# HGRN scores of each level as products of 64 or 32 keys with their own queries

## The chip, the cores and the metric

The kernel runs on one core of a Trainium2 chip. The metric is the device time of one execution in microseconds, as the median of several runs. Before the change it is 2824.28 us (three runs, 2824.19 to 2826.57).

## What is computed

A trunk of two layers over 256 tokens of 2048 features in float32: a gated DeltaNet layer, a SwiGLU feed-forward layer, an HGRN2 layer and a second feed-forward layer. The change lies in the HGRN2 token mixer, in the scores of its chunks:

```python
# q, k, logf: (B,S,H,dk), 16 heads of 128; chunks of 64 tokens
qc, kc, vc = to_chunks(q), to_chunks(k), to_chunks(v.astype(jnp.float32))
Bc = jnp.cumsum(to_chunks(logf), axis=-2)
def step(S, inp):
    q_c, k_c, v_c, b_c, qd_c, kd_c, fl_c = inp
    dec = jnp.exp(jnp.where(causal, b_c[..., :, None, :] - b_c[..., None, :, :], -jnp.inf))
    scores = jnp.einsum("bhid,bhjd,bhijd->bhij", q_c, k_c, dec)
    o = jnp.einsum("bhid,bhde->bhie", qd_c, S) + jnp.einsum("bhij,bhje->bhie", scores, v_c)
    S = S * fl_c[..., :, None] + jnp.einsum("bhjd,bhje->bhde", kd_c, v_c)
    return S, o
```

The decay differs by channel, so a score is not a plain product of a query and a key; it needs a factor in each channel that depends on both positions.

## The kernel before

**The stream of weights.** All weights pass through the core once, in half chunks of 128x1024. SP loads a half (`raw`), ScalarE rounds it (`wh`), VectorE takes the rest (`wl`), and TensorE multiplies three products of the parts with the activations. These matmuls write the PSUM tiles `main`. Four buffers each hold `raw`, `wh` and `wl`.

**The work beside it.** The token mixers' own matmuls are in plain float32 and write PSUM tiles `aux`, of which there are four (one bank each). The profile shows a float32 matmul as two pairs of a weight load and a matmul; such a pair is called a record below. The page gives most instructions one line, L489, since a recording layer issues them; so they are told apart by their tiles.

**What sets the order.** The program is recorded first. A planner (`Recorder.plan`) then places operations engine by engine: the stream's matmuls keep their order, and the other matmuls are put between them when their operands should be ready by a table of costs (`COST`, `PE_SLACK`, `FP32_PRODUCT`). `batches` keeps the matmuls of one `aux` tile, or of tiles declared `together`, in one piece. Each engine then runs its instructions in that order.

**HGRN scores.** The 16 heads come in four groups of four. For a group, `hgrn_scores` takes the 256 tokens as two blocks of 128 per head (eight pairs of head and block). Pairs of a later query and an earlier key are covered by levels `s` = 64, 32, 16, 8, 4, 2 and 1: at level `s` a block of 2s tokens has its keys in the first half and its queries in the second, and with `b` at the last key as reference both factors are plain exponentials. `products` makes `kp` (keys times the factor), `qp` (queries times the factor) and one matmul for each head and block of 128. At levels 64 and 32 the keys are packed to 64 columns; at levels 16, 8, 4 and 2 all 128 keys are multiplied with all 64 queries. `keep` copies what belongs together into `sc` (keys in partitions, eight blocks, queries): ScalarE by slices at levels 64 and 32, VectorE with a mask (`copy_predicated`) below. Level 1 and the diagonal (each query with its own key) come from one product of 128 keys with 64 + 128 columns `q_last`, in four `aux` tiles. `hgrn_o` multiplies `v` by `sc`.

Two levels form one piece for the planner, so a group has three stretches on TensorE: levels 64 and 32; levels 16 and 8; levels 4, 2 and 1 with the diagonal.

Of the kernel before, what the change touches and what calls it, by code (L numbers as in the profile page):

```python
# [11 lines left out]
AF = mybir.ActivationFunctionType  # L12
ALU = mybir.AluOpType
# [4 lines left out]
P = 128  # L18
T = 256
D = 2048  # L20
EPS = 1e-6
CH = 64
# [3 lines left out]
N_HGRN = 4  # L26
LEVELS = (64, 32, 16, 8, 4, 2, 1)
MASKED = LEVELS[2:]
AHEAD = 3
RAW_BUFS = 4  # L30
SPLIT_BUFS = 4
# [474 lines left out]
class Trunk:  # L506
# [79 lines left out]
    def stream(self, groups):  # L586
# [10 lines left out]
        def load(n):  # L597
            g, i = flat[n]
            raw = self.tile(self.wraw, [P, 1024], "raw", ordered=True)
            nc.sync.dma_start(raw, g.halves[i])  # L600
            if n == 0:
                nc.ops[-1].lag = 4.2
                nc.edge(self.queue[1], nc.ops[-1])
            h = place("wh", g)
            nc.scalar.activation(h, raw, AF.Copy)
            low = place("wl", g)
            nc.vector.tensor_tensor(out=low, in0=raw, in1=h.bitcast(F32), op=ALU.subtract)
            ready[n] = (h, low)

        loaded = 0  # L610
        for n, (g, i) in enumerate(flat):
            while loaded < min(n + AHEAD, len(flat)):
                load(loaded)
# [730 lines left out]
    def hgrn_setup(self):  # L1344
# [4 lines left out]
        nc.gpsimd.dma_start(self.hgrn_hn, a["hgrn_hn"])  # L1349
        self.masks = t([P, len(MASKED), CH], "masks", U8)  # L1350
        raw = self.tile(self.pool, [P, len(MASKED), CH], "e", bufs=2, ordered=True)
        nc.gpsimd.dma_start(raw, a["masks"])
# [56 lines left out]
    def hgrn_scores(self, g, q, st):  # L1409
        nc = self.nc  # L1410
        t = lambda shape, tag, **kw: self.tile(self.pool, shape, tag, **kw)
        b, k = st["b"], st["k"]
        e = t([P, 4, T], "e", bufs=2, ordered=True)
        nc.scalar.activation(e, q, AF.Tanh, scale=0.5)
        nc.vector.scalar_tensor_tensor(
            out=q, in0=e, scalar=1.0, in1=q, op0=ALU.add, op1=ALU.mult
        )
        tt = lambda out, in0, in1, op: nc.vector.tensor_tensor(out=out, in0=in0, in1=in1, op=op)
        halves = lambda x, s: x.rearrange("p h (n t s) -> p (h n) t s", t=2, s=s)
        flat = lambda x: x.rearrange("p h t -> p (h t)")  # L1420


        e, kp, qp = t([P, 4, T], "e", bufs=2, ordered=True), self.kp[0], t([P, 4, P], "qp", bufs=2, ordered=True)
        ch = lambda x, c: x[:, :, c * CH : (c + 1) * CH]
        tot = lambda c: b[:, :, (c + 1) * CH - 1 : (c + 1) * CH].broadcast_to([P, 4, CH])
        tt(ch(e, 0), tot(0), ch(b, 0), ALU.subtract)
        tt(ch(e, 0), ch(e, 0), tot(1), ALU.add)
        tt(ch(e, 1), tot(1), ch(b, 1), ALU.subtract)
        nc.vector.tensor_copy(ch(e, 2), ch(b, 2))
        tt(ch(e, 3), ch(b, 3), tot(2), ALU.add)  # L1430
        nc.scalar.activation(e, e, AF.Exp)
        tt(kp[:, :, 0:P], k[:, :, 0:P], e[:, :, 0:P], ALU.mult)
        tt(qp, q[:, :, P:T], e[:, :, P:T], ALU.mult)
        ps = self.aux()
        for h in range(4):
            nc.tensor.matmul(
                ps[:, h * P : (h + 1) * P], kp[:, h, 0:P], qp[:, h, :], start=True, stop=True
            )
        cross = t([P, 512], "cross")
        nc.scalar.activation(cross, ps, AF.Copy)  # L1440
        st["cross"] = cross

        sc = t([P, 8, P], "sc")
        nc.gpsimd.memset(sc, 0.0)

        def products(n, s, ps):
            e, qp = t([P, 4, T], "e", bufs=2, ordered=True), t([P, 4, P], "qp", bufs=2, ordered=True)
            bv, ev, kv, qv = (halves(x, s) for x in (b, e, k, q))
            m, whole, kp = 512 // s, s not in MASKED, self.kp[(n + 1) % 2]
            if whole:  # L1450
                kp = flat(kp)[:, 0:512]
                left = kp.rearrange("p (m s) -> p m s", s=s)
            else:
                left = halves(kp, s)[:, :, 0, :]
            ref = bv[:, :, 0, s - 1 : s].broadcast_to([P, m, s])
            tt(ev[:, :, 0, :], ref, bv[:, :, 0, :], ALU.subtract)
            if s == CH:
                nc.scalar.activation(ev[:, :, 0, :], ev[:, :, 0, :], AF.Exp)
                nc.scalar.activation(ev[:, :, 1, :], bv[:, :, 1, :], AF.Exp)
            else:  # L1460
                tt(ev[:, :, 1, :], bv[:, :, 1, :], ref, ALU.subtract)
                nc.scalar.activation(e, e, AF.Exp)
            tt(left, kv[:, :, 0, :], ev[:, :, 0, :], ALU.mult)
            tt(qp.rearrange("p h (n s) -> p (h n) s", s=s), qv[:, :, 1, :], ev[:, :, 1, :], ALU.mult)
            for h in range(4):
                for tok in range(2):
                    at = (2 * h + tok) * CH
                    keys = kp[:, at : at + CH] if whole else kp[:, h, tok * P : (tok + 1) * P]
                    nc.tensor.matmul(
                        ps[0 : CH if whole else P, at : at + CH], keys,  # L1470
                        qp[:, h, tok * CH : (tok + 1) * CH], start=True, stop=True,
                    )

        def keep(n, s, ps):
            pv = ps.rearrange("p (a n s) -> p a n s", a=8, s=s)
            if s not in MASKED:
                for i in range(CH // s):
                    nc.scalar.activation(
                        sc[2 * i * s : (2 * i + 1) * s, :, (2 * i + 1) * s : (2 * i + 2) * s],
                        pv[i * s : (i + 1) * s, :, i, :], AF.Copy,  # L1480
                    )
            else:
                nc.vector.copy_predicated(
                    sc.rearrange("p a (n t s) -> p a n t s", t=2, s=s)[:, :, :, 1, :],
                    self.masks[:, n - 2, :].rearrange("p (n s) -> p n s", s=s).unsqueeze(1)
                    .broadcast_to([P, 8, CH // s, s]),
                    pv,
                )

        for n in range(0, len(LEVELS) - 1, 2):  # L1490
            two = self.aux(), self.aux()
            nc.together(*two)
            for step in (products, keep):
                for i in range(2):
                    step(n + i, LEVELS[n + i], two[i])


        e, qp = t([P, 4, T], "e", bufs=2, ordered=True), t([P, 8, CH + P], "q_last")
        pairs = lambda x: x.rearrange("p h (a n t) -> p (h a) n t", a=2, t=2)
        bv, ev, qv = (pairs(x) for x in (b, e, q))  # L1500
        nc.gpsimd.tensor_copy(qp[:, :, CH:], q.rearrange("p h (a t) -> p (h a) t", t=P))
        tt(ev[:, :, :, 1], bv[:, :, :, 1], bv[:, :, :, 0], ALU.subtract)
        nc.scalar.activation(ev[:, :, :, 1], ev[:, :, :, 1], AF.Exp)
        tt(qp[:, :, 0:CH], qv[:, :, :, 1], ev[:, :, :, 1], ALU.mult)
        mask = lambda m: m.unsqueeze(1).broadcast_to([P, 2, m.shape[1]])
        pv = []
        for h in range(4):
            if h % 2 == 0:
                two = self.aux(), self.aux()
                nc.together(*two)  # L1510
            pv.append(two[h % 2][:, 0 : 2 * (CH + P)].rearrange("p (a i) -> p a i", a=2))
            for tok in range(2):
                nc.tensor.matmul(
                    pv[h][:, tok, :], k[:, h, tok * P : (tok + 1) * P], qp[:, 2 * h + tok, :],
                    start=True, stop=True,
                )
        for h in range(4):
            out = sc[:, 2 * h : 2 * h + 2, :]
            nc.vector.copy_predicated(
                out.rearrange("p a (n t) -> p a n t", t=2)[:, :, :, 1],  # L1520
                mask(self.masks[:, len(MASKED) - 1, :]), pv[h][:, :, 0:CH],
            )
            nc.vector.copy_predicated(out, mask(self.same), pv[h][:, :, CH:])
        st["sc"] = sc

    def hgrn_o(self, g, st):
# [128 lines left out]
def layout(inputs):  # L1655
# [33 lines left out]
    def out_rows(w):  # L1689
# [20 lines left out]
    out["masks"] = np.stack(  # L1710
        [((j >= c // s * 2 * s) & (j < c // s * 2 * s + s)).astype(np.float32) for s in MASKED], 1
    )
# [21 lines left out]
```

## Time and profile before

| What | Value |
|---|---|
| median of three runs | 2824.28 us |
| the profiled execution's own time | 2823.72 us |
| its span on the page | 2822.0 us |
| granted TensorE clock | 0.999 |
| DMA moved | 580.46 MB, 206 GB/s in the mean |
| SyncE and GpSimd | POOL busy 253.7 us; the loads' queue 53.9% of the DMA engines' span |
| HGRN stage | 1574 to about 2000 us of the span |

An instruction row of the timeline is: start in us, length in us, engine, line, operation, output tile <- input tiles, array tile (rows*columns), shape, and how many alike follow each other. The length of such a run ends with its last record's own latency, so starts are compared rather than ends. In a group row the busy time is a union, behind it the mean length in ns.

### The profile page before, as it was taken

The numbers are of one execution on the slowest core, as the hardware profiler recorded it, in microseconds if no ns is written. First come the engines' busy times: TensorE is split into PE (matmuls) and PEld (weight loads), VectorE is DVE, ScalarE is ACT, GpSimd is POOL, SyncE is SP. The second block draws the span as 40 slices with busy tenths as digits, with TensorE's granted clock in tenths as the row PEclk, the third lists the DMA queues.
The fourth block names the chain that finished last, engine by engine and source line by source line (L and its number), as shares of the span: only waits on it lengthen the run. The fifth ranks groups of instructions, "written<-read, shape, count | busy, mean of one in ns | idle before, by whom it ended". The sixth has DMA issues, their size and how long they took to land.

```text
span 2822.0 us, 39791 instructions
## 1 busy us (share of the span) xinstructions
PE 2806.4 (99%) x15198; PEld 2398.8 (85%) x15198; DVE 1745.9 (62%) x2511; ACT 1420.5 (50%) x1972; POOL 253.7 (9%) x370
## 2 busy tenths in 40 slices
PE   9999999999999999999999999999999999999998
PEld 9988888888888888888888989999888888888887
DVE  6787888877665545445555677677565455445554
ACT  6646666564554444344444555556454444344443
POOL 1212222222110000000000100000110000000000
PEclk9999999999999999999999999999999999999999
DMA  7686668668676555665556644544685556665554
GB/s 258 194 277 205 205 221 260 213 206 267 229 254 196 187 192 188 223 224 187 193 187 224 209 151 165 165 150 165 223 268 187 193 188 204 225 205 193 187 198 160
DMA packets 162672, 580.46 MB, mean 206 GB/s; under 512 B 20138, under 2 KB 21306, under 8 KB 162352
## 3 DMA queue, kind: packets, MB, share of 16 engines
q1 hardware_dynamic: 138912, 503.15, 53.9%
q0 software_dynamic: 23280, 73.91, 8.3%
q8 instruction: 119, 1.95, 0.3%
q10 hardware_dynamic: 288, 0.85, 0.1%
q14 instruction: 73, 0.60, 0.1%
HBM read 550.52 MB, written 27.31 MB: 205 GB/s over the span
## 4 chain that ended last, share of the span: by engine, by line
PE 98%; ACT 0%; DVE 0%; issue 0%; DMA 0%; SPq 0%; POOLq 0%; POOL 0%; ACTq 0%
PE main L489 90%; PE aux L489 8%; ACT dec L489 0%; DMA first<-in_x 0%; DVE wl L489 0%; DVE u L489 0%; ACT wh L489 0%; DVE utmp L489 0%; DVE pre L489 0%; SPq L489 0%; ACT xt_h L489 0%; ACT y L489 0%; POOLq L1730 0%; ACT junk L489 0%; DVE xl L489 0%
## 5 line engine op out<-in xcount | busy, mean ns | idle before, releaser
L489 DVE TENSOR_TENSOR wl<-raw,wh 128x1024 fp32r<-128x1024 f32 x945 | 1162.3, 1231 | 973.9 <-ACT wh L489 971.4
L489 ACT ACTIVATE wh<-raw 128x1024 fp32r<-128x1024 f32 x945 | 1000.6, 1060 | 1287.1 <-PE main L489 1238.9
L489 PE MATMUL main<-wh,xt_h 128*128 128x512 f32 x2176 | 850.7, 391 | 0.6 <-ACT wh L489 0.6
L489 PE MATMUL main<-wl,xt_h 128*128 128x512 f32 x2176 | 849.2, 390 | 0.9 <-DVE wl L489 0.9
L489 PE MATMUL main<-wh,xt_l 128*128 128x512 f32 x2176 | 849.4, 390 | 0.0
L489 PEld LDWEIGHTS main<-wl,xt_h 128*128 128x128 f32 x2176 | 408.7, 188 | 84.3 <-DVE wl L489 1.3
L489 PEld LDWEIGHTS main<-wh,xt_h 128*128 128x128 f32 x2176 | 408.7, 188 | 84.2 <-ACT wh L489 1.0
L489 PEld LDWEIGHTS main<-wh,xt_l 128*128 128x128 f32 x2176 | 408.7, 188 | 83.6
L489 PE MATMUL main<-xt_h,wl 128*128 128x256 f32 (+1 forms) x1040 | 292.3, 281 | 1.1 <-DVE wl L489 1.1
L489 PE MATMUL main<-xt_l,wh 128*128 128x256 f32 (+1 forms) x1040 | 291.9, 281 | 0.3 <-DVE xt_l L489 0.3
L489 PE MATMUL main<-xt_h,wh 128*128 128x256 f32 (+1 forms) x1040 | 290.1, 279 | 0.0
L489 PE MATMUL main<-wh,hth 128*128 128x512 f32 x664 | 258.7, 390 | 0.0
L489 PE MATMUL main<-wh,htl 128*128 128x512 f32 x664 | 258.6, 389 | 0.0
L489 PE MATMUL main<-wl,hth 128*128 128x512 f32 x664 | 258.4, 389 | 0.0
L489 PEld LDWEIGHTS main<-xt_h,wh 128*128 128x128 f32 (+1 forms) x1040 | 195.7, 188 | 0.3
L489 PEld LDWEIGHTS main<-xt_h,wl 128*128 128x128 f32 (+1 forms) x1040 | 193.8, 186 | 1.6 <-DVE wl L489 1.5
L489 PEld LDWEIGHTS main<-xt_l,wh 128*128 128x128 f32 (+1 forms) x1040 | 193.8, 186 | 0.9 <-DVE xt_l L489 0.5
L489 PE MATMUL main<-wl,ot_h 128*128 128x512 f32 x384 | 150.8, 393 | 0.0
L489 PE MATMUL main<-wh,ot_l 128*128 128x512 f32 x384 | 150.6, 392 | 0.0
L489 PE MATMUL main<-wh,ot_h 128*128 128x512 f32 x384 | 150.5, 392 | 0.0
L489 PEld LDWEIGHTS main<-wh,htl 128*128 128x128 f32 x664 | 124.7, 188 | 25.9
L489 PEld LDWEIGHTS main<-wl,hth 128*128 128x128 f32 x664 | 124.7, 188 | 25.8
(207 smaller groups left out, 2236.4 us busy)
## 6 DMA issues: line engine op xcount, KB each, us to landing
raw<-in_ffn_gu SPq DMA_DIRECT2D x352, 512.0 KB, 3.7
raw<-in_ffn_d SPq DMA_DIRECT2D x176, 512.0 KB, 4.4
raw<-in_hgrn_in SPq DMA_DIRECT2D x128, 512.0 KB, 3.7
raw<-in_gdn_kq SPq DMA_DIRECT2D x64, 512.0 KB, 5.1
raw<-in_gdn_v SPq DMA_DIRECT2D x64, 512.0 KB, 4.5
raw<-in_gdn_z SPq DMA_DIRECT2D x64, 512.0 KB, 4.9
raw<-in_gdn_out SPq DMA_DIRECT2D x64, 512.0 KB, 4.6
x_home<-x POOLq DMA_DIRECT2D x36, 512.0 KB, 5.9
```

Source lines behind the costliest of these rows:

```text
L489: getattr(getattr(tc.nc, op.eng), op.method)(*args, **kw)
```

## The change

For levels 16 and 8 each head's block of 128 keys is cut in two blocks of 64, for levels 4 and 2 in four blocks of 32 (`BLOCK`). Each block of keys is multiplied with only its own queries (half as many as keys), and the result is written at the PSUM partitions of those keys, so consecutive matmuls write to partitions 0 and 64, or 0, 32, 64 and 96. At levels 64 and 32 the products stay as they are, but the second block of 128 tokens writes to partitions 64 to 127. Level 1 and the diagonal become products of 32 keys with 16 + 32 columns, all in one `aux` tile where four were used. The copies into `sc` are cut by the same blocks.

```diff
+BLOCK = {16: 64, 8: 64, 4: 32, 2: 32}
...
             for h in range(4):
                 for tok in range(2):
-                    at = (2 * h + tok) * CH
-                    keys = kp[:, at : at + CH] if whole else kp[:, h, tok * P : (tok + 1) * P]
-                    nc.tensor.matmul(
-                        ps[0 : CH if whole else P, at : at + CH], keys,
-                        qp[:, h, tok * CH : (tok + 1) * CH], start=True, stop=True,
-                    )
+                    if whole:
+                        at = (2 * h + tok) * CH
+                        nc.tensor.matmul(
+                            ps[tok * CH : (tok + 1) * CH, h * CH : (h + 1) * CH], kp[:, at : at + CH],
+                            qp[:, h, tok * CH : (tok + 1) * CH], start=True, stop=True,
+                        )
+                        continue
+                    w = BLOCK[s]
+                    for j in range(P // w):
+                        nc.tensor.matmul(
+                            ps[j * w : (j + 1) * w, (2 * h + tok) * w // 2 : (2 * h + tok + 1) * w // 2],
+                            kp[:, h, tok * P + j * w : tok * P + (j + 1) * w],
+                            qp[:, h, tok * CH + j * w // 2 : tok * CH + (j + 1) * w // 2],
+                            start=True, stop=True,
+                        )
...
+                for tok in range(2):
+                    for i in range(CH // s):
+                        nc.scalar.activation(
+                            to[2 * i * s : (2 * i + 1) * s, :, tok, (2 * i + 1) * s : (2 * i + 2) * s],
+                            pv[tok * CH + i * s : tok * CH + (i + 1) * s, :, i, :], AF.Copy,
+                        )
+                return
+            w = BLOCK[s]
+            for j in range(P // w):
+                b = slice(j * w, (j + 1) * w)
+                masked(b, s, n - 2, ps[b, 0 : 4 * w].rearrange("p (a n s) -> p a n s", a=8, s=s))
+
+        def masked(b, s, at, pv):
+            w = b.stop - b.start
+            nc.vector.copy_predicated(
+                sc[b, :, b].rearrange("p a (n t s) -> p a n t s", t=2, s=s)[:, :, :, 1, :],
+                self.masks[b, at, b.start // 2 : b.stop // 2].rearrange("p (n s) -> p n s", s=s)
+                .unsqueeze(1).broadcast_to([w, 8, w // 2 // s, s]),
+                pv,
+            )
...
-        e, qp = t([P, 4, T], "e", bufs=2, ordered=True), t([P, 8, CH + P], "q_last")
+        e, qp = t([P, 4, T], "e", bufs=2, ordered=True), t([P, 8, 4, 48], "q_last")
...
+        ps = self.aux()
         for h in range(4):
-            if h % 2 == 0:
-                two = self.aux(), self.aux()
-                nc.together(*two)
-            pv.append(two[h % 2][:, 0 : 2 * (CH + P)].rearrange("p (a i) -> p a i", a=2))
             for tok in range(2):
-                nc.tensor.matmul(
-                    pv[h][:, tok, :], k[:, h, tok * P : (tok + 1) * P], qp[:, 2 * h + tok, :],
-                    start=True, stop=True,
-                )
+                a = 2 * h + tok
+                for j in range(4):
+                    nc.tensor.matmul(
+                        ps[32 * j : 32 * j + 32, a * 48 : a * 48 + 48],
+                        k[:, h, tok * P + 32 * j : tok * P + 32 * j + 32], qp[:, a, j, :],
+                        start=True, stop=True,
+                    )
+        pv = ps[:, 0:384].rearrange("p (a i) -> p a i", a=8)
+        for j in range(4):
+            b = slice(32 * j, 32 * j + 32)
+            masked(b, 1, len(MASKED) - 1, pv[b, :, 0:16].unsqueeze(3))
             nc.vector.copy_predicated(
-                out.rearrange("p a (n t) -> p a n t", t=2)[:, :, :, 1],
-                mask(self.masks[:, len(MASKED) - 1, :]), pv[h][:, :, 0:CH],
-            )
-            nc.vector.copy_predicated(out, mask(self.same), pv[h][:, :, CH:])
+                sc[b, :, b], self.same[b, b].unsqueeze(1).broadcast_to([32, 8, 32]), pv[b, :, 16:]
+            )
```

The planner places the new pieces anew. The rows below are of the first group; numbers behind names are those of buffers, and a row ends with the output's shape (partitions x columns) and its count.

TensorE, levels 16 and 8, before:

```order
L489 MATMUL main_14770<-wl_14721,xt_h_12_68 128x512
L489 MATMUL aux_14799<-qp_14742,kp_2270_13975 128x64 x7
L489 MATMUL aux_14813<-qp_14774,kp_2269_13974 128x64
L489 MATMUL aux_14799<-qp_14742,kp_2270_13975 128x64
L489 MATMUL aux_14813<-qp_14774,kp_2269_13974 128x64 x7
L489 MATMUL main_14770<-wh_14702,xt_l_16_72 128x512
```

The same place now:

```order
L490 MATMUL main_14773<-wl_14697,xt_h_12_68 128x512
L490 MATMUL aux_14778<-qp_14743,kp_2270_13975 64x32 x9
L490 MATMUL aux_14794<-qp_14757,kp_2269_13974 64x32
L490 MATMUL aux_14778<-qp_14743,kp_2270_13975 64x32
...
L490 MATMUL aux_14794<-qp_14757,kp_2269_13974 64x32 x9
L490 MATMUL main_14773<-wh_14680,xt_l_16_72 128x512
```

Sixteen matmuls become 32. The row with x9 alternates between partitions 0 and 64; where the two levels take turns, two matmuls in a row go to the same partitions (0, 0, 64, 64). The piece stands 12 stream matmuls earlier: 20 instead of 32 lie between levels 64 and 32 and this one.

TensorE, levels 4, 2 and 1, before:

```order
L489 MATMUL main_14770<-wl_14765,xt_h_13_69 128x512
L489 MATMUL aux_14858<-qp_14824,kp_2270_13975 128x64 x3
L489 MATMUL aux_14862<-qp_14829,kp_2269_13974 128x64
...
L489 MATMUL aux_14862<-qp_14829,kp_2269_13974 128x64 x3
L489 MATMUL aux_14880<-q_last_13985,k_13978 128x192
L489 MATMUL aux_14882<-q_last_13985,k_13978 128x192
...
L489 MATMUL main_14770<-wh_14751,xt_l_17_73 128x512
L489 MATMUL main_14770<-wh_14751,xt_h_13_69 128x512
L489 MATMUL aux_14890<-q_last_13985,k_13978 128x192
L489 MATMUL aux_14893<-q_last_13985,k_13978 128x192
```

The same place now:

```order
L490 MATMUL main_14773<-wh_14753,xt_h_13_69 128x512
L490 MATMUL aux_14870<-q_last_13985,k_13978 32x48 x32
L490 MATMUL aux_14908<-qp_14829,kp_2270_13975 32x16 x3
L490 MATMUL aux_14912<-qp_14842,kp_2269_13974 32x16
...
L490 MATMUL aux_14912<-qp_14842,kp_2269_13974 32x16 x3
L490 MATMUL main_14773<-wl_14769,xt_h_13_69 128x512
```

Sixteen and eight matmuls become 64 and 32, and consecutive ones go to different partitions of 0, 32, 64 and 96 throughout. The piece follows levels 16 and 8 after 26 stream matmuls instead of 18.

VectorE, the copies into `sc` of the first group, before:

```order
L489 TENSOR_TENSOR kp_2269_13974<-k_13978,e_14784 128x256x2
L489 COPY_PREDICATED sc_13983<-masks_13997,aux_14799 128x32x16
L489 TENSOR_TENSOR q_last_13985<-q_13980,e_14834 128x8x64
L489 TENSOR_TENSOR wl_14855<-raw_14738,wh_14846 128x1024
L489 COPY_PREDICATED sc_13983<-masks_13997,aux_14813 128x64x8
L489 COPY_PREDICATED sc_13983<-masks_13997,aux_14858 128x128x4
L489 COPY_PREDICATED sc_13983<-masks_13997,aux_14862 128x256x2
L489 COPY_PREDICATED sc_13983<-masks_13997,aux_14880 128x128
...
L489 COPY_PREDICATED sc_13983<-same_13999,aux_14893 128x256
L489 TENSOR_TENSOR wl_14915<-raw_14779,wh_14903 128x1024
```

The same place now:

```order
L490 TENSOR_TENSOR kp_2269_13974<-k_13978,e_14790 128x256x2
L490 TENSOR_TENSOR wl_14862<-raw_14709,wh_14850 128x1024
L490 COPY_PREDICATED sc_13983<-masks_13997,aux_14794 64x8x4x8
L490 TENSOR_TENSOR wl_14888<-raw_14738,wh_14865 128x1024
L490 COPY_PREDICATED sc_13983<-masks_13997,aux_14794 64x8x4x8
L490 COPY_PREDICATED sc_13983<-masks_13997,aux_14908 32x8x4x4 x4
L490 COPY_PREDICATED sc_13983<-masks_13997,aux_14912 32x8x8x2 x4
L490 COPY_PREDICATED sc_13983<-masks_13997,aux_14870 32x8x16
L490 TENSOR_TENSOR wl_15003<-raw_14783,wh_14992 128x1024
L490 COPY_PREDICATED sc_13983<-masks_13997,aux_14870 32x8x16 x3
L490 COPY_PREDICATED sc_13983<-same_13999,aux_14870 32x8x32
L490 TENSOR_TENSOR wl_15026<-raw_14816,wh_15012 128x1024
```

Twelve masked copies of a group become twenty, and halves of the weight stream now stand between them. On TensorE 45 stream matmuls lie between the end of the last piece and the first use of `wl_15003`.

More of the change, by code (lines that the diff above doesn't have):

```diff
@@ L1474, in keep @@
+                    w = BLOCK[s]
[6 more added lines that the diff above has]
+                        )
         def keep(n, s, ps):
-            pv = ps.rearrange("p (a n s) -> p a n s", a=8, s=s)
@@ L1476, in keep @@
             if s not in MASKED:
[L1477 to L1480, printed above, removed]
-                    )
[L1482 to L1487, printed above, removed]
-                )
+                pv = ps[:, 0:T].rearrange("p (h n s) -> p h n s", h=4, s=s)
@@ new lines, in keep @@
+                to = sc.rearrange("p (h t) q -> p h t q", t=2)
+                for tok in range(2):
[9 more added lines that the diff above has]
+                masked(b, s, n - 2, ps[b, 0 : 4 * w].rearrange("p (a n s) -> p a n s", a=8, s=s))
@@ L1495, in hgrn_scores @@
                     step(n + i, LEVELS[n + i], two[i])
-        e, qp = t([P, 4, T], "e", bufs=2, ordered=True), t([P, 8, CH + P], "q_last")
+        e, qp = t([P, 4, T], "e", bufs=2, ordered=True), t([P, 8, 4, 48], "q_last")
         pairs = lambda x: x.rearrange("p h (a n t) -> p (h a) n t", a=2, t=2)
         bv, ev, qv = (pairs(x) for x in (b, e, q))
-        nc.gpsimd.tensor_copy(qp[:, :, CH:], q.rearrange("p h (a t) -> p (h a) t", t=P))
+        blocks = lambda x: x.rearrange("p a (j n) -> p a j n", j=4)
@@ L1502, in hgrn_scores @@
+        nc.gpsimd.tensor_copy(qp[:, :, :, 16:], q.rearrange("p h (a j n) -> p (h a) j n", a=2, j=4))
         tt(ev[:, :, :, 1], bv[:, :, :, 1], bv[:, :, :, 0], ALU.subtract)
         nc.scalar.activation(ev[:, :, :, 1], ev[:, :, :, 1], AF.Exp)
-        tt(qp[:, :, 0:CH], qv[:, :, :, 1], ev[:, :, :, 1], ALU.mult)
-        mask = lambda m: m.unsqueeze(1).broadcast_to([P, 2, m.shape[1]])
-        pv = []
+        tt(qp[:, :, :, 0:16], blocks(qv[:, :, :, 1]), blocks(ev[:, :, :, 1]), ALU.mult)
+        ps = self.aux()
@@ L1507, in hgrn_scores @@
         for h in range(4):
-            if h % 2 == 0:
-                two = self.aux(), self.aux()
-                nc.together(*two)
-            pv.append(two[h % 2][:, 0 : 2 * (CH + P)].rearrange("p (a i) -> p a i", a=2))
             for tok in range(2):
-                nc.tensor.matmul(
-                    pv[h][:, tok, :], k[:, h, tok * P : (tok + 1) * P], qp[:, 2 * h + tok, :],
-                    start=True, stop=True,
-                )
-        for h in range(4):
-            out = sc[:, 2 * h : 2 * h + 2, :]
+                a = 2 * h + tok
```

## The prediction

> **What bounds the kernel now.** I read the page first, part 1 and the chain of part 4, then TensorE's waits.
>
> ```profile
> PE 2806.4 (99%) x15198; PEld 2398.8 (85%) x15198; DVE 1745.9 (62%) x2511; ACT 1420.5 (50%) x1972; POOL 253.7 (9%) x370
> PE 98%; ACT 0%; DVE 0%; issue 0%; DMA 0%; SPq 0%; POOLq 0%; POOL 0%; ACTq 0%
> ```
>
> ```profile
> PE main L489 <- DVE wl L489: 2.0, 2, 1.1
> ```
>
> TensorE is busy for 99% of the span and 98% of the chain is its own work; its longest sum of waits is 2.0 us. So TensorE time is kernel time, and every microsecond that a stretch of score matmuls gives up should appear in the result, if nothing else becomes late. What the stretches cost is read from the timeline. First the pace of the weight stream, 30 records from the first of these rows to the second:
>
> ```profile
> 1619.84 0.39 PE L489 MATMUL main<-wh,xt_l 128*128 128x512 f32 x1
> ...
> 1626.41 0.39 PE L489 MATMUL main<-wl,xt_h 128*128 128x512 f32 x1
> ```
>
> (1626.41 - 1619.84) / 29 = 0.227 us a record. A stretch's price is then the time between a stream record ahead of it and the second one behind it, less two such steps (0.45 us). The second is taken because the first one behind a stretch is itself late. The three stretches of the first group:
>
> ```profile
> 1635.70 0.39 PE L489 MATMUL main<-wh,xt_l 128*128 128x512 f32 x1
> 1636.02 2.08 PE L489 MATMUL aux<-qp,kp 128*64 128x64 f32 x32
> 1638.03 0.50 PE L489 MATMUL main<-wh,xt_h 128*128 128x512 f32 x1
> 1638.36 0.39 PE L489 MATMUL main<-wl,xt_h 128*128 128x512 f32 x1
> ...
> 1645.19 0.39 PE L489 MATMUL main<-wl,xt_h 128*128 128x512 f32 x1
> 1645.42 3.68 PE L489 MATMUL aux<-qp,kp 128*128 128x64 f32 x32
> 1648.90 0.48 PE L489 MATMUL main<-wh,xt_l 128*128 128x512 f32 x1
> 1649.22 0.39 PE L489 MATMUL main<-wh,xt_h 128*128 128x512 f32 x1
> ...
> 1652.89 0.39 PE L489 MATMUL main<-wl,xt_h 128*128 128x512 f32 x1
> 1653.12 3.68 PE L489 MATMUL aux<-qp,kp 128*128 128x64 f32 x32
> 1656.63 1.52 PE L489 MATMUL aux<-q_last,k 128*128 128x192 f32 x8
> 1657.85 0.53 PE L489 MATMUL main<-wh,xt_l 128*128 128x512 f32 x1
> 1658.22 0.40 PE L489 MATMUL main<-wh,xt_h 128*128 128x512 f32 x1
> 1658.45 1.46 PE L489 MATMUL aux<-q_last,k 128*128 128x192 f32 x8
> 1659.62 0.53 PE L489 MATMUL main<-wl,xt_h 128*128 128x512 f32 x1
> 1659.98 0.39 PE L489 MATMUL main<-wh,xt_l 128*128 128x512 f32 x1
> ```
>
> Levels 64 and 32: 2.66 - 0.45 = 2.21 us. Levels 16 and 8: 4.03 - 0.45 = 3.58. Levels 4, 2 and 1: (5.33 - 0.45) + (1.76 - 0.45) = 6.19. Together 11.98 us a group, 47.9 us for the four, which is all that the change can touch on TensorE.
>
> **What a record costs.** Two stretches of the first layer give the law for smaller array tiles:
>
> ```profile
> 199.28 0.39 PE L489 MATMUL main<-wh,xt_h 128*128 128x512 f32 x1
> 199.60 0.69 PE L489 MATMUL aux<-inv,nmat 32*32 32x32 f32 x32
> 200.23 0.50 PE L489 MATMUL main<-wl,xt_h 128*128 128x512 f32 x1
> 200.56 0.40 PE L489 MATMUL main<-wh,xt_l 128*128 128x512 f32 x1
> ...
> 207.55 0.39 PE L489 MATMUL main<-wh,xt_l 128*128 128x512 f32 x1
> 207.87 1.14 PE L489 MATMUL aux<-inv,nmat 64*64 64x64 f32 x16
> 208.94 0.50 PE L489 MATMUL main<-wh,xt_h 128*128 128x512 f32 x1
> 209.28 0.39 PE L489 MATMUL main<-wl,xt_h 128*128 128x512 f32 x1
> ```
>
> The 16 records of 64 columns cost 1.73 - 0.45 = 1.28 us, the 32 of levels 64 and 32 cost 2.21: (2.21 - 1.28) / 16 = 0.058 us a record, and 2.21 - 32 x 0.058 = 0.35 us for entering and leaving the small tiles. With full tiles it is 3.58 / 32 = 0.112 and nothing fixed. So the price follows the key columns, not the 64 queries, and 32 columns should cost 0.029 alone. The 32 records of 32*32 cost 1.28 - 0.45 = 0.83, less 0.35, 0.015 us each: half of that. In the code (`gdn_inverse`) they alternate between two tiles that share neither rows nor columns of the array. Two such tiles run side by side. A record of `q_last` (192 moving columns) costs (4.88 - 3.58) / 8 = 0.163, 1.45 times the 0.112: the larger of key columns and query columns counts.
>
> **The change, part by part.** No row shows two tiles that share all 128 rows and differ in columns alone, which is what the change makes. From both sides: nothing side by side (0.058 and 0.029 a record), or as many at once as there are tiles (two of 64: 0.029; four of 32: 0.007). I take two at a time for both widths (0.029 and 0.015), since 0.015 is the densest pace that a row shows.
>
> - Levels 64 and 32, still 32 records: 32 x 0.029 + 0.35 = 1.28, so -0.93.
> - Levels 16 and 8, 64 records: 64 x 0.029 + 0.35 = 2.21, so -1.37. Where the order takes partitions 0, 0, 64, 64, some of this may be lost.
> - Levels 4 and 2, 128 records at 0.015 = 1.92; level 1 and the diagonal, 64 records with 48 queries over 32 columns, 1.5 x 0.015 = 0.0225, 1.44; with 0.35 this is 3.71, so -2.48.
>
> That is -4.78 a group, -19.1 us in all. [...]
>
> VectorE has twenty masked copies a group instead of twelve.
>
> ```profile
> L489 DVE COPY_PREDICATED sc<-masks,aux 128x512 f32<-128x512 uint8 x16 | 13.7, 855 | 5.8 <-PE aux L489 5.4
> L489 DVE COPY_PREDICATED sc<-same,aux 128x256 f32<-128x256 uint8 x16 | 6.4, 457 | 0.0
> L489 DVE COPY_PREDICATED sc<-masks,aux 128x128 f32<-128x128 uint8 x16 | 5.9, 451 | 1.9 <-PE aux L489 1.6
> ```
>
> Now they cost (13.7 + 6.4 + 5.9) / 4 = 6.5 us a group; each partition copies as many elements as before, so the lower end is +0, and with 0.46 for each of twenty it is 9.2, +2.7. Behind the last piece VectorE has nine of them and one weight half ahead of `wl_15003`, 9 x 0.46 + 1.23 = 5.4 us, while TensorE has 45 stream matmuls, 45 x 0.227 = 10.2 us. That cover holds; without it up to 2.7 us a group would show. ScalarE's copies into `sc`:
>
> ```profile
> L489 ACT ACTIVATE sc<-aux 32x256 f32<-32x256 f32 x8 | 3.0, 372 | 0.9 <-PE aux L489 0.8
> L489 ACT ACTIVATE sc<-aux 64x512 f32<-64x512 f32 x4 | 2.4, 590 | 1.0 <-PE aux L489 0.9
> ```
>
> One of 512 and two of 256 elements become two of 256 and four of 128; by the slope (590 - 372) / 256 a 128 takes about 0.26, so 1.33 becomes 1.79 us a group. ScalarE is idle half the span, which hides it. GpSimd's copy to `q_last` and the loads of SP keep their number and order.
>
> The waits. VectorE is the engine to be late:
>
> ```profile
> 1620.00:1640.00 20.00, 20.00 (x116) 16.70 (x116) 18.93 (x24) 12.60 (x16) 1.03 (x1) 1.00 0.58 189
> 1640.00:1660.00 20.00, 20.00 (x127) 18.19 (x126) 15.73 (x24) 7.83 (x9) 0.00 (x0) 1.00 0.31 107
> ```
>
> Busy for 18.93 and 15.73 of 20 us, it prepares `kp`, `qp` and `q_last` while TensorE now reaches the pieces sooner: 26 matmuls (5.9 us) plus 2.21 after the start of levels 16 and 8, where before it was 3.58 plus 18 x 0.227 = 7.7. If the operands of the last piece are late, that wait blocks everything behind it on TensorE. No such wait is there now; 8.1 against 7.7 us says none is added, but two of the copies now stand ahead of `kp` (2 x 0.46), and the piece before it ends sooner. I take 0.5 us a group, 2 us in all, between 0 and 1.5.
>
> The sum: 2823.72 - 19.1 + 2.0 = 2806.6 for the profiled execution, which lay 0.56 under the median: **2807 us**.
>
> **The rivals.**
>
> *Four at once.* If all four 32-column tiles run together, the last stretch is (1.92 + 1.44) / 2 + 0.35 = 2.03, so -4.16, and a group -6.46. That is -25.8 + 2 us: 2800.5 by the median, 2798.5 without the waits. For it: 0.015 is what two tiles make, each at its own 0.029. Against it: no row is denser than 0.015.
>
> *A floor under the pace.* If records can't follow each other that densely for long, the last stretch with its 192 records suffers. At 0.030 beyond the first 32 it is 0.48 + 4.8 + 0.35 = 5.63, and the sum about -2.8 a group, 2815 with the waits; at 0.035 it is about -1.9, 2819, some more with longer waits. [...] The trace's mean of 0.015 in two tiles speaks against it.
>
> *Nothing side by side.* The 32*32 tiles may overlap because their rows differ; here all tiles use all rows. Then levels 64 and 32 stay at 2.21, levels 16 and 8 take 64 x 0.058 + 0.35 = 4.06 (+0.48), and the last 128 x 0.029 + 64 x 0.0435 + 0.35 = 6.85 (+0.66): +1.1 a group, 2829. This is also the case in which the change doesn't do what it says. [...]
>
> *The instruction feed, slower than before.* The longest dense run in the trace is 32 records; the last stretch now has 192 in one piece. If TensorE's sequencer brings a record only every r us once the queued ones are used up, the stretch costs 0.48 + 160 r + 0.35, and levels 16 and 8 0.93 + 32 r + 0.35. It decides from r = 0.045, where both and the -0.93 add up to nothing. At 0.058, the slowest pace that rows of small tiles show, they are 10.11 (+3.92) and 3.13 (-0.45): +2.5 a group, 2834. For it: none of the rows excludes it. Against it: 32 records at 0.015 without a slowing. [...]
>
> **How the numbers follow.** Two at a time: 0.42, 2803 to 2812. Four at once: 0.27, down to 2797. A floor under the pace: 0.12, up to 2822. Nothing side by side: 0.11, 2826 to 2833. The feed: 0.08, above 2834. The range 2797 to 2822 leaves out the last two, 0.19. About 0.2% (5.6 us) is what a measurement of this kernel can tell from no change. Faster, below 2818.6: 0.42 + 0.27 + 0.09 = 0.78. Same: 0.03 of the floor and 0.08 of the third rival, 0.11. Slower: 0.03 + 0.08 = 0.11.
>
> **What would show it.** In the new timeline the first stretch must shrink from 2.21 to about 1.3 us and the second from 3.58 to 2.2; if both stay at 2.2 and 4.1, nothing runs side by side. The last stretch tells 2.0 (four), 3.7 (two), 5 to 6 (a floor) and 10 (the feed) apart; in the last case its first records are dense and the later ones are not. TensorE's waits should stay under 2 us more than now, on VectorE's `kp` or `q_last`; more would make the prediction wrong on the side of VectorE. The masked copies should total 6.5 to 9.2 us a group.

## The result, and the profile after

| | before | after |
|---|---|---|
| median of four runs each, us | 2824.24 | 2810.32 |
| lowest to highest, us | 2823.88 to 2826.57 | 2808.67 to 2811.66 |
| the profiled execution, us | 2823.72 | 2811.11 |
| its span, us | 2822.0 | 2809.4 |

The ratio is 0.9947, with a 95% interval of 0.9935 to 0.9959: 13.9 us faster. The forecast was 2807 us, between 2797 and 2822.

The page of the changed kernel, part 1:

```profile
PE 2788.2 (99%) x15902; PEld 2376.0 (85%) x15902; DVE 1752.2 (62%) x2543; ACT 1422.0 (51%) x1984; POOL 255.1 (9%) x370
```

TensorE still is the bound. It issues 704 records more and is busy for 18 us less. Its waits in the changed kernel (what it waited for, us in all, how often, the longest):

```profile
PE aux L490 <- issue: 6.2, 4, 2.0
```

The row is new: four waits for nothing that the profile shows, 6.2 us in all. No row names `kp` or `q_last`.

The stretches of the first group, in the timeline of TensorE:

```profile
1637.94 0.39 PE L490 MATMUL main<-wh,xt_l 128*128 128x512 f32 x1
1638.26 1.15 PE L490 MATMUL aux<-qp,kp 128*64 128x64 f32 x32
1639.34 0.50 PE L490 MATMUL main<-wh,xt_h 128*128 128x512 f32 x1
1639.68 0.39 PE L490 MATMUL main<-wl,xt_h 128*128 128x512 f32 x1
...
1643.78 0.39 PE L490 MATMUL main<-wl,xt_h 128*128 128x512 f32 x1
1644.10 2.08 PE L490 MATMUL aux<-qp,kp 128*64 128x32 f32 x64
1646.11 0.50 PE L490 MATMUL main<-wh,xt_l 128*128 128x512 f32 x1
1646.44 0.39 PE L490 MATMUL main<-wh,xt_h 128*128 128x512 f32 x1
...
1651.91 0.39 PE L490 MATMUL main<-wh,xt_h 128*128 128x512 f32 x1
1652.23 0.89 PE L490 MATMUL aux<-q_last,k 128*32 128x48 f32 x64
1652.99 1.17 PE L490 MATMUL aux<-qp,kp 128*32 128x16 f32 x108
1656.17 0.38 PE L490 MATMUL aux<-qp,kp 128*32 128x16 f32 x20 [2.01 <-issue]
1656.48 0.50 PE L490 MATMUL main<-wl,xt_h 128*128 128x512 f32 x1
1656.82 0.39 PE L490 MATMUL main<-wh,xt_l 128*128 128x512 f32 x1
```

With the same rule as in the prediction (from the stream record ahead to the second one behind, less 0.45 us):

- Levels 64 and 32: 1.74 - 0.45 = **1.29 us**, 2.21 before.
- Levels 16 and 8: 2.66 - 0.45 = **2.21**, 3.58 before. The places where the order takes partitions 0, 0, 64, 64 cost nothing that shows: 2.21 is the sum forecast without them.
- Levels 4, 2, 1 and the diagonal: 4.91 - 0.45 = **4.46**, 6.19 before. The records themselves are far denser than forecast: 64 of `q_last` start within 1652.99 - 1652.23 = 0.76 us, 0.012 each. But after 172 of the 192 records TensorE stands still for 2 us, with nothing named that it waits for.

The other groups have such a stop too, in their own places of the same stretch:

```profile
1756.89 0.49 PE L490 MATMUL aux<-qp,kp 128*32 128x16 f32 x31 [1.67 <-issue]
...
1859.07 0.18 PE L490 MATMUL aux<-qp,kp 128*32 128x16 f32 x1 [1.93 <-issue]
...
1960.45 0.18 PE L490 MATMUL aux<-qp,kp 128*32 128x16 f32 x1 [0.56 <-issue]
```

Behind the second and the third stop the clock falls for a while. The windows view of the changed kernel (the third number from the right is the granted clock):

```profile
1740.00:1760.00 20.00, 18.34 (x334) 15.21 (x329) 17.86 (x30) 10.12 (x16) 0.00 (x0) 0.95 0.47 150
1760.00:1780.00 20.00, 20.00 (x110) 17.36 (x110) 11.76 (x18) 10.35 (x24) 2.59 (x2) 0.96 0.42 130
...
1860.00:1880.00 20.00, 20.00 (x95) 16.76 (x94) 12.54 (x23) 8.25 (x21) 2.59 (x2) 0.91 0.39 127
```

0.09 x 20 us = 1.8 us are lost in the last of them, as many in the first two together. Until the last microseconds of the span, the records of the clock show three stretches of 3.41 us at 0.5: from 242.66, 1758.18 and 1860.58 us.

Comparing when the same stream record starts in both kernels gives the whole account of the profiled execution. The four groups gain 4.06, 2.87, 2.48 and 5.45 us, together 14.86; 0.59 is lost at the start and 1.67 at 242 us, where TensorE waits for `wl` in both kernels (0.93 us before, 0.94 after) and only in the changed one the clock drops behind it. That leaves 12.6, which is 2823.72 - 2811.11. The drop at 242 us is no property of the scores: of the eight kernels below four have it in their profiled execution (the split one, the two with 64 keys at levels 4 and 2, the one moved by 84) and four have not, so single executions differ by these 1.67 us for a reason far from the change.

### The profile page after: what moved, and what is told of

Same layout as the page of the kernel before. It is cut to its first block, busy times and chain, and to the rows that moved or that the text cites. A ratio compares the mean times of both kernels' runs of the same rounds, so it can differ in the third digit from the quotient of the medians.

```text
span 2809.4 us, 41241 instructions
## 1 busy us (share of the span) xinstructions
PE 2788.2 (99%) x15902; PEld 2376.0 (85%) x15902; DVE 1752.2 (62%) x2543; ACT 1422.0 (51%) x1984; POOL 255.1 (9%) x370
## 3 DMA queue, kind: packets, MB, share of 16 engines
q8 instruction: 124, 2.03, 0.3%
## 4 chain that ended last, share of the span: by engine, by line
PE 98%; issue 0%; ACT 0%; DVE 0%; POOLq 0%; POOL 0%; ACTq 0%
PE main L490 91%; PE aux L490 7%; ACT dec L490 0%; DVE wl L490 0%; ACT wh L490 0%; DVE u L490 0%; ACT xt_h L490 0%; DVE utmp L490 0%; DVE pre L490 0%; ACT y L490 0%; POOLq L1748 0%; ACT junk L490 0%; DVE xl L490 0%; POOL coll L490 0%; DVE xt_l L490 0%
## 5 line engine op out<-in xcount | busy, mean ns | idle before, releaser
L490 PEld LDWEIGHTS main<-wh,hth 128*128 128x128 f32 x664 | 124.7, 188 | 25.8
```

Source lines behind the costliest of these rows:

```text
L490: getattr(getattr(tc.nc, op.eng), op.method)(*args, **kw)
```

## The experiments

The times of before are from runs on the same chip in the same session: 2824.64 us beside the split kernel, the one moved by 44 records, the one with the first two stretches alone and the one with 64 keys at levels 4 and 2; 2823.95 beside the one moved by 84 records; 2824.38 beside the other three.

Two theories stood at the start. **A**: the instructions arrive in blocks, and a dense stretch uses one up before the next is there. **B**: the stop belongs to the stretch itself, its length, its PSUM tile or its operands.

**The last stretch in two parts.** `nc.after(sc)` keeps what follows behind the copies into `sc` recorded so far, so that 14 stream matmuls come between levels 4 and 2 and the last piece:

```diff
         ps = self.aux()
+        nc.after(sc)
         for h in range(4):
             for tok in range(2):
                 a = 2 * h + tok
```

> The products of level 1 and the diagonal are held back behind the copies of levels 4 and 2, so that the last stretch of 192 records becomes one of 128 and one of 64 with stream matmuls between; all else as changed. Theory (the instruction feed comes in blocks of 256 instructions, and a block that is used up in about 1.5 us leaves TensorE without instructions until the next one has landed): no gap in either piece, 128 x 0.0083 + 0.35 = 1.4 us and 64 x 0.011 + 0.35 = 1.05 us in place of 4.46 with its gap, no half-clock stretches of 3.4 us behind the gaps: 2810.3 - 4 x 2.0 - 3.4 = about 2799 us. Rival (the gap is a wait for an operand that VectorE makes late): the gap stays ahead of or in the later piece, since VectorE has the same work, 2808 to 2812 us.

Measured 2801.95 us, ratio 0.9917 (0.9904 to 0.9931). Its timeline of TensorE, group 1:

```profile
1651.97 0.39 PE L490 MATMUL main<-wl,xt_h 128*128 128x512 f32 x1
1652.29 1.32 PE L490 MATMUL aux<-qp,kp 128*32 128x16 f32 x128
1653.54 0.50 PE L490 MATMUL main<-wh,xt_l 128*128 128x512 f32 x1
1653.88 0.40 PE L490 MATMUL main<-wh,xt_h 128*128 128x512 f32 x1
...
1658.23 0.39 PE L490 MATMUL main<-wl,xt_h 128*128 128x512 f32 x1
1658.55 0.89 PE L490 MATMUL aux<-q_last,k 128*32 128x48 f32 x64
1659.36 0.50 PE L490 MATMUL main<-wh,xt_l 128*128 128x512 f32 x1
1659.70 0.40 PE L490 MATMUL main<-wh,xt_h 128*128 128x512 f32 x1
```

1.91 - 0.45 = 1.46 us and 1.47 - 0.45 = 1.02, no stop, no row with "issue" among the waits. Every group gains 6.0 us (11.98 - 1.29 - 2.21 - 1.46 - 1.02). So neither the copies by block nor the tile sizes hold the gain back. The same work in shorter dense pieces gives 8.4 us more than the change as it was made; about 11 more were expected, because a stop of 2.0 us was reckoned for each group and the fourth had one of 0.56.

**The whole program moved by 44 records.** The warm-up at the start gets 22 more, but narrow, products; nothing else differs:

```diff
-        for i in range(10):
+        for i in range(32):
             self.nc.tensor.matmul(
-                warm[:, (i % 4) * P : (i % 4 + 1) * P], self.ones, self.ones, start=True, stop=True
+                warm[0:8, 0:8], self.ones[:, 0:8], self.ones[:, 0:8], start=True, stop=True
             )
```

> Nothing of the scores differs from the changed kernel. At the very start, where TensorE waits for the input, 32 warm-up matmuls of 8 columns stand for the ten of 128 columns, so every later TensorE instruction stands 88 places further on. Theory: the boundary of an instruction block, which the changed kernel meets after 172 of the first group's 192 records, is met after 128, and the boundary ahead of it at the stretch's first record, so that the next block is asked for while stream matmuls still run; the gaps vanish or shrink in most groups, 2800 to 2805 us. Rivals (a wait for an operand, or a sequencer that can't hold the pace for more than about 100 to 170 records): the place of an instruction in the program doesn't matter, the gaps stay at the same records and the time stays at 2810 us.

Measured 2803.43 us, ratio 0.9924 (0.9910 to 0.9937). One stop is left, in group 1:

```profile
1654.33 0.77 PE L490 MATMUL aux<-qp,kp 128*32 128x16 f32 x64 [1.11 <-issue]
```

It stands behind record 128 of the stretch instead of 172, 44 records earlier, and is shorter. The groups without a stop gain 6.2 to 6.3 us. The four groups together gain 8.9 us more than in the changed kernel; another 1.67 come from the drop at 242 us, which this execution doesn't have, and 1.2 are lost again elsewhere ahead of the groups.

**Moved by 84 records**, the same edit with 52 warm-up products.

> The changed kernel with 52 warm-up products of 8 columns at the start in place of 10 of 128: 42 products more, so all later TensorE instructions stand 168 places (84 records) further on; nothing else differs. Theory A (TensorE runs out of instructions at fixed places 256 apart, and a gap there is the longer the more dense records ran since the last block came): the gap of group 1, at record 172 of its last stretch in the changed kernel and at 128 with a shift of 88, stands at record 88, if it is still to be seen; by the step from 2.01 to 1.11 us for 44 records it falls to about 0.2 us; the time is 2800 to 2806 us, with another group's gap coming in where its stretch has moved onto an edge (1 to 2 us, and 1.7 more for a half-clock stretch). Theory B (the gap belongs to the stretch, its copies or its buffers): gaps stay at 172 records or so and 2811 us.

Measured 2807.22 us, ratio 0.9938 (0.9922 to 0.9955). Group 1 has no stop; the others have one of 0.63, 0.92 and 2.02 us, two of them no longer in the stretch but in the stream behind it:

```profile
1759.05 0.39 PE L490 MATMUL main<-wh,xt_l 128*128 128x512 f32 x1 [0.63 <-issue]
...
1956.73 0.18 PE L490 MATMUL aux<-qp,kp 128*32 128x16 f32 x1 [2.02 <-issue]
```

The place of the record behind each stop, counted over all of TensorE's recorded matmuls (my own count from the trace):

```text
changed kernel   9398   10291   11184   12077
moved by 44      9398
moved by 84             10419   11312   12205
```

Moving the program by 44 records leaves the count of the first stop where it was, and the other stops after a move by 84 are at the old counts plus 128 each. A record is two instructions (the page counts 15902 weight loads and 15902 matmuls), so those stops moved by 0 and by 256 instructions where the work moved by 88 and by 168. The four of the changed kernel are 893 records apart, and the trace shows six more instructions of TensorE (EVENT_SEMAPHORE) in each of the three distances: 2 x 893 + 6 = 1792, seven times 256. That settles A against B. The expected size for group 1 (0.2 us) came out as nothing to be seen, and the time within 2800 to 2806 was missed by 1.2 us; in the three other groups a stop came in or stayed.

What comes in blocks can be read in part 3 of the page, the queue of TensorE's instructions, before and after (packets, MB, share):

```profile
q8 instruction: 119, 1.95, 0.3%
```

```profile
q8 instruction: 124, 2.03, 0.3%
```

2.03 MB / 124 is 16 KB a packet. TensorE's records are 2 x 15902 = 31804 instructions, 256.5 for each of the 124 packets (30396 / 119 = 255.4 before), so a packet holds about 256 of them, the step that the places of the stops show. In the mean one starts for every 128 records, though not evenly where records are dense. Around the four stops (start and length of the packet, when TensorE stops, when it goes on, from the single packets in the trace):

```text
1653.55  1.12   1653.98  1656.17
1754.62  0.98   1755.05  1756.89
1856.72  0.97   1856.93  1859.07
1958.21  0.96   1959.69  1960.45
```

TensorE goes on 1.3 to 1.5 us after such a packet has landed, about 2.2 to 2.6 us after it was started. The packet was started close to the record that stands 128 ahead of the stop (from 0.2 us before that record ran to 1.1 us after it), so, as I read it, only about one block was in hand; from that record until TensorE goes on it is 2.0 to 3.5 us. At the stream's 0.227 us for two instructions a block lasts 29 us and hides this; in the dense stretches the 128 records ahead of the four stops lasted 1.2 to 1.3 us.

**Only the first two stretches.** `BLOCK` keeps 128 keys for levels 4 and 2, and the last piece is as before the change (the edit also puts back its code, left out here).

```diff
-BLOCK = {16: 64, 8: 64, 4: 32, 2: 32}
+BLOCK = {16: 64, 8: 64, 4: 128, 2: 128}
```

> Only the first half of the change: levels 64 and 32 at alternating partitions and levels 16 and 8 in blocks of 64; levels 4, 2 and 1 with the diagonal are as before the change. Theory: no gap, and the two terms of the prediction alone, 4 x (0.93 + 1.37) = 9.2 us: 2815 us. Rival (the copies by block or the new places of the stretches cost something of their own, hidden in the sum): 2818 us or more.

Measured 2814.92 us, ratio 0.9967 (0.9954 to 0.9979); each group gains 2.26 to 2.32 us, where 0.93 + 1.37 = 2.30 was forecast.

**Levels 4 and 2 with 64 keys.**

```diff
-BLOCK = {16: 64, 8: 64, 4: 32, 2: 32}
+BLOCK = {16: 64, 8: 64, 4: 64, 2: 64}
```

> Levels 4 and 2 in blocks of 64 keys with 32 queries, as levels 16 and 8, instead of 32 with 16: 64 records for 128. Theory: the last stretch has 128 records, 64 x 0.029 + 64 x 0.011 + 0.35 = 2.9 us, and takes no gap, since a block of instructions now lasts longer: 2810.3 - 4 x 1.55 - 3.4 = about 2801 us. Rival (wait for an operand): 2.9 us plus the same gap of about 2 us, 4.9 against 4.46 now, so 2811 to 2813 us.

Measured 2824.82 us, ratio 0.9998 (0.9989 to 1.0006): no gain at all, which neither theory expected. Groups 1 and 2 are as expected (5.5 us each), but groups 3 and 4 lose 4.7 and 5.2. Group 3 in its timeline:

```profile
1852.27 0.46 PE L490 MATMUL aux<-q_last,k 128*32 128x48 f32 x24
1852.66 0.77 PE L490 MATMUL aux<-qp,kp 128*64 128x32 f32 x18
1853.36 0.27 PE L490 MATMUL aux<-q_last,k 128*32 128x48 f32 x2
1853.56 0.30 PE L490 MATMUL aux<-qp,kp 128*64 128x32 f32 x2
1853.80 0.27 PE L490 MATMUL aux<-q_last,k 128*32 128x48 f32 x2
...
1863.03 0.39 PE L490 MATMUL aux<-q_last,k 128*32 128x48 f32 x8
1863.35 0.80 PE L490 MATMUL main<-wl,xt_h 128*128 128x512 f32 x1
```

The planner put products of 32 keys and of 64 keys in turns of two or four records. A turn of two costs 0.20 to 0.24 us, where two records beside their like cost 0.02 to 0.06, and the stretch takes 11.1 us, where that of group 1, with one change of size in it, takes 2.8. From 1857.1 us on the clock is at 0.5 for 10.2 us (0.74 in the mean from 1850 to 1870), and again in group 4 (0.50 from 1970 to 1980).

**The same, with the last piece held back.** The edits of the split kernel and of this one together.

> Levels 4 and 2 as products of 64 keys, and the last piece's products held behind the copies of levels 4 and 2, so that 64-key and 32-key products cannot be mixed in one stretch. Theory A (what cost the 64-key kernel its gain was that in two groups its 64-key and 32-key products stood in turns of two, at 0.20 to 0.24 us a turn, with the clock halved during it): levels 4 and 2 cost 2.2 us a group as levels 16 and 8 do, the last piece 1.0 as in the split kernel, 3.2 against that kernel's 2.5, so 2801.95 + 4 x 0.75 = about 2805 us, and no half-clock stretch in the four groups. Theory B (64-key products of levels 4 and 2 cost more by themselves, or draw the clock down): 2815 to 2825 us, with half-clock stretches left.

Measured 2805.06 us, ratio 0.9931 (0.9918 to 0.9945); groups gain 5.2 to 5.3 us and no clock drop is left in them. So 64 keys cost no more than their records do; the loss came with the mixed sizes. In the kernel moved by 84 records `q_last` and `qp` are mixed too, both in tiles of 32 columns:

```profile
1852.53 0.37 PE L490 MATMUL aux<-qp,kp 128*32 128x16 f32 x21
1852.74 0.21 PE L490 MATMUL aux<-q_last,k 128*32 128x48 f32 x1
1852.74 0.18 PE L490 MATMUL aux<-qp,kp 128*32 128x16 f32 x1
...
1854.40 0.26 PE L490 MATMUL aux<-q_last,k 128*32 128x48 f32 x3
```

All 192 records are through in 1.9 us there: one size of tile, no price for the turns.

**One tile after the other.** On the split kernel, levels 64 and 32 run all products of one column tile before the other's, and the last piece takes the blocks `j` in the outer loop (the part for levels 64 and 32 is left out here):

```diff
...
-        for h in range(4):
-            for tok in range(2):
-                a = 2 * h + tok
-                for j in range(4):
+        for j in range(4):
+            for h in range(4):
+                for tok in range(2):
+                    a = 2 * h + tok
...
```

> As the split kernel, but levels 64 and 32 go through all products of one column tile before the other, and the last piece through all eight products of each tile in turn. Theory A (only neighbours in the order that stand in different tiles run beside each other): levels 64 and 32 cost 2.2 us as in the kernel before, not 1.29; the last piece runs at 0.0425 us a record (four records in 42.5 ns is one turn of a tile), so 64 records take 2.7 us and the stretch about 2.9, not 1.02; 4 x (0.92 + 1.9) = 11 us more than the split kernel, about 2813 us. Theory B (the engine works on the tiles each by itself, whatever the order): 2802 us and both stretches as in the split kernel.

Measured 2808.45 us, ratio 0.9943 (0.9929 to 0.9957).

```profile
1656.02 0.39 PE L490 MATMUL main<-wl,xt_h 128*128 128x512 f32 x1
1656.34 2.49 PE L490 MATMUL aux<-q_last,k 128*32 128x48 f32 x64
1658.76 0.50 PE L490 MATMUL main<-wh,xt_l 128*128 128x512 f32 x1
1659.10 0.39 PE L490 MATMUL main<-wh,xt_h 128*128 128x512 f32 x1
```

The last piece costs 3.08 - 0.45 = 2.63 us, 1.02 in alternation, and levels 64 and 32 cost 1.67 instead of 1.29. Within a tile the records start 42 to 43 ns apart. Both prices are somewhat under those expected (2.9 and 2.2), because at each change of tile four or five records do run beside those of the other. So theory A of that run holds with a small reach: here TensorE ran tiles side by side only for records that stood a few places apart in its order.

**All masked levels with 32 keys**, on the split kernel.

```diff
-BLOCK = {16: 64, 8: 64, 4: 32, 2: 32}
+BLOCK = {16: 32, 8: 32, 4: 32, 2: 32}
```

> As the split kernel, with levels 16 and 8 too as products of 32 keys: 128 records of 128x16 at four tiles in place of 64 records of 128x32 at two. If four tiles run at once wherever they stand: the stretch falls from 2.2 us to about 1.5 (the split kernel's stretch of levels 4 and 2 is 1.46), 4 x 0.75 = 3 us less, about 2799 us. If the end of an instruction block falls into one of the eight stretches of 128 dense records: 1 to 2 us more for each hit, and 1.7 us for each half-clock stretch behind it, so 2800 to 2806 us with waits put down to issue; the engine's sequence is as far along at group 1 as before, since the stretches ahead of it are alike.

Measured **2798.70 us**, ratio 0.9908 (0.9895 to 0.9922), the best of all.

```profile
1641.43 0.39 PE L490 MATMUL main<-wl,xt_h 128*128 128x512 f32 x1
1641.75 1.31 PE L490 MATMUL aux<-qp,kp 128*32 128x16 f32 x128
1642.99 0.50 PE L490 MATMUL main<-wh,xt_l 128*128 128x512 f32 x1
1643.33 0.39 PE L490 MATMUL main<-wh,xt_h 128*128 128x512 f32 x1
```

1.90 - 0.45 = 1.45 us for levels 16 and 8, 0.76 less than with 64 keys. But the first three groups gain only 0.5 us more than in the split kernel. There the first product of `v` and `sc` starts 0.41 us after the stream record ahead of it, 0.23 in the split kernel: now with 24 masked copies a group, VectorE ends the last copy into `sc` only 0.15 us before it, so these copies are no longer hidden. One stop of 0.49 us is left, in the stream of group 4. The four groups give 1.4 of the 4.3 us between the two profiled executions; 1.67 are the drop at 242 us, which only the split kernel's has, and 1.2 were gained at the start. So the time met its expectation of 2799 us in part by luck.

## Why the prediction was right, and where it was not

- **TensorE is the bound, so its time is the kernel's time**: right. The gain read from the starts of stream records is the gain of the profiled execution.
- **Levels 64 and 32** (-0.93 a group): right, -0.92. **Levels 16 and 8** (-1.37): right, -1.37. Two tiles of 64 columns that share all 128 rows do run side by side, and run e3 shows both terms alone. That rules out the rival with nothing side by side, which put the two stretches at 2.21 and 4.06. It rules out the floor under the pace too, since in the split kernel 128 records followed each other at 9 ns in the mean ((1.32 - 0.18) / 127 us).
- **Levels 4, 2, 1 and the diagonal** (-2.48): this is the step that failed, and in two ways that partly cancelled. "I take two at a time for both widths" was wrong for 32 columns: four run at once. In the moved kernels, groups with no stop gain 6.2 to 6.3 us, against the 6.46 of the four-at-once rival. The premise that 0.015 us was as dense as it gets came from rows in which only two tiles took turns. But the stretch also holds more records than one block of instructions, and the stops and the clock behind them took 2.3, 3.5, 3.9 and 0.9 us of 6.33 from the four groups, 10.5 us in all. What remains of the term is -1.77 in group 1 and about -1.4 in the mean.
- **The feed.** The rival had the right resource and the wrong shape: a slower pace from the 33rd record on, to be seen as dense first records and slow later ones. The trace has neither. The pace stays at 9 to 12 ns to the edge of a block, and then nothing comes for up to 2 us. A price per record could not have given this; it depends on where in the program the stretch stands.
- **The waits** (+0.5 a group on VectorE's operands): there are none in the groups. **The copies**: the three groups of masked copies and the two of ScalarE that the change makes are

```profile
L490 DVE COPY_PREDICATED sc<-masks,aux 32x128 f32<-32x128 uint8 x48 | 18.8, 391 | 5.4 <-PE aux L490 4.0
L490 DVE COPY_PREDICATED sc<-same,aux 32x256 f32<-32x256 uint8 x16 | 7.1, 444 | 0.5
L490 DVE COPY_PREDICATED sc<-masks,aux 64x256 f32<-64x256 uint8 x16 | 6.9, 431 | 0.3
L490 ACT ACTIVATE sc<-aux 32x128 f32<-32x128 f32 x16 | 4.3, 269 | 0.2
L490 ACT ACTIVATE sc<-aux 64x256 f32<-64x256 f32 x8 | 3.0, 374 | 0.0
```

32.8 / 4 = 8.2 us a group on VectorE (6.5 to 9.2 forecast) and 1.83 on ScalarE (1.79). All of it is hidden in this kernel.

So the forecast of 2807 lay 3.3 us from the time, but not for the reason that it gave: the four groups gained 14.9 us where 19.1 - 2.0 = 17.1 stood, and 2.3 us were lost outside them. That the total came so close is luck: what four tiles at once gained over two (about 1.6 us a group) was taken back by stops that nobody had reckoned with.

## What to carry to other kernels

Cut products to the keys that they need, spread them over all column tiles of one size, and let neighbours in the order stand in different tiles; mixed sizes (2824.82 us here) gave the whole gain back, one tile after another (2808.45 against 2801.95) a part of it. Keep a dense piece no longer than a block of instructions (128 records here), with longer matmuls between pieces: the same products in pieces of 128 and 64 records gained 22.7 us where one piece of 192 gained 13.9. With three such pieces in a group, two of them of 128 records, one stop of 0.49 us came back, so shorter is safer. A wait that the profile puts down to "issue" and that moves when unrelated instructions are added at the start of the program, as here from record 172 of the stretch to 128, points to the feed.

## What the runs showed of the hardware

- Four tiles of 32 columns over all 128 rows ran at once: in the changed kernel four records of 48 query columns took 42.5 ns together, as long as one alone took in its tile when one tile came after the other (42 to 43 ns).
- TensorE's instructions came in packets of 16 KB, about 256 instructions each (31804 / 124); where a dense stretch used one up before the next was there, TensorE stood still for 0.49 to 2.02 us.
- The drops of the clock to 0.5 lasted 3.41 us each in the changed kernel, and 10.2 us with 64 keys at levels 4 and 2. Those of the changed kernel start 1515.5 and 102.4 us apart, 444.0 and 30.0 times the 3.413 us that the trace gives for each. The two in the groups start 1.3 and 1.5 us after the end of a stop of 1.67 and of 1.93 us; the one at 242.66 us follows waits of 0.60 us for `wh` and 0.94 us for `wl`. But behind the stop of 2.01 us in group 1 the clock stayed at 1.00, and with 64 keys at levels 4 and 2 the drops came without a stop, amid the turns of sizes. What brings the clock down is not shown.
